# Attention values in one fp32r pass, the last branch's gates first, and wide weight splits in a hybrid encoder block

## The chip, the cores and the metric

One core of one Trainium2 chip runs the whole kernel. The metric is device microseconds of one execution, the median of several runs. Matrix products run on PE (TensorE); DVE (VectorE) and ACT (ScalarE) do the elementwise work, POOL (GpSimd) a few sums and some DMA issues, SP (SyncE) most DMA issues.

## The reference

The input is 512 tokens of width 1024 and 256 memory tokens. One layer computes

```
h = rms_norm(x);  proj = h @ w_in            # q,k,v,o,gates | na q,k,v | xa q | merge gates
y_ml = bidirectional mLSTM (4 heads of 128)
y_na = neighbourhood attention (8 heads of 64) on the 8 x 64 token grid, with a 2-D bias
y_xa = cross-attention into the memory tokens (4 heads of 128)
merged = g_ml*(y_ml @ w_br_ml) + g_na*(y_na @ w_br_na) + g_xa*(y_xa @ w_br_xa)
x = x + merged @ w_out
x = x + conv_glu_ffn(rms_norm(x))            # width 2816
return rms_norm(x)
```

All in float32. In the neighbourhood attention each token sees the 8 grid rows and a window of 16 of the 64 columns: scores, bias, softmax, and then `o = p @ v` (the "values" below).

## The kernel before

**Three passes.** A product of float32 tiles appears in the trace as two matmul records, one of fp32r tiles (a rounded format) as one. Nearly every product is made in fp32r of split operands: a number is the sum of a rounded high part and the low rest, and `mm3` (line 201) adds high by high, high by low and low by high. Activations are split by `split_act` (206: ACT copies the high part, line 208, DVE subtracts, 209).

**Weights.** All weights lie in one flat array in the order of `block_list` (53). A block is 512 KB as a rule (1024 columns on 128 partitions) and serves one projection of 24 matmuls of 512 columns (`proj`, 332). `weights(key)` (190) loads three blocks ahead on SP's queue and splits one block ahead: `emit_split` (167) makes two halves of 512 columns, each with one ACT copy (184) and one DVE subtraction (185), into four buffers of 544 columns for the high and four for the low parts.

**Order.** The kernel is written as one stream of projections; between them `step` (833) advances generators that hold the attention branches: `ml_all` (538), `xa_all` (754) and `na_all` (647), the neighbourhood attention. A compile-time scheduler orders each engine's instructions, by readiness and program order, so the engines' queues are fixed before the run. Pools are fixed too: 15 "units" of 2064 columns, 7 scratch tiles, 4 PSUM banks for projections (`mm`) and 4 for the attention (`at`).

**The branch loop (line 904).** For each of three branches, eight gate projections `("g", br, f)` (scaled by DVE at 919, tanh on ACT at 920) and four branch blocks `("br", br, fp)` of two outputs each, in the order gate, gate, branch block; gates are multiplied in at 935 and 937, summed at 938. `RATE` (31) says how many generator steps go with each: 0.85 in branch 0, 1.6 in branch 1, 0 in branch 2. `na_all` is appended when branch 1 begins; `drain` (900) runs what is left of a generator before the branch block that needs it.

**The neighbourhood attention.** Its values come out of the time-major projections at 414: in rounds c = 2 and 3 ACT copies them scaled into four scratch tiles (436), which go to a DRAM tensor `nav_d` (512 x 512) in four DMAs on POOL's queue (438). `load_vwin` (441) loads them back, once for all heads, as eight windows (4 column windows by 2 halves of the rows) of 32 partitions times 4 pieces: 32 DMAs of 64 KB on POOL's queue (448), into two units. `na_all` then has 16 tasks, one for each head and pair of column windows. Step t runs `scores` of task t (fp32r: QS and QZ by KS, 687 and 688; bias and maximum on DVE at 692; exp on ACT, 697; reciprocal; the normalising product on DVE, 699), then `values` of task t - 2, then `transposes` of task t - 1 (four float32 transposes, 705, and one copy of 128x512 out of PSUM, by ACT at 708 for even tasks and DVE at 710 for odd ones). `values` (713) makes four float32 products of 128 columns (718). After every second task `store` (720) copies the head's 64x512 result as high part (ACT, 726) and low part (DVE, 727). `prep` (654) splits q and k of two heads before every fourth task.

After the branches come the output projection (`out`), and the FFN in two halves of eleven up-blocks (`ua` with a convolution and a tanh gelu, `uu`) and eight down-blocks (`dn`).

Of the kernel before, what the change touches and what calls it, by code (L numbers as in the profile page):

```python
# [17 lines left out]
P = 128  # L18
S = 512
# [11 lines left out]
RATE = (0.85, 1.6, 0)  # L31
# [3 lines left out]
HWD = 544  # L35
# [17 lines left out]
def block_list():  # L53
# [13 lines left out]
    for br in range(3):  # L67
        for fp in range(4):
            L.append((("g", br, 2 * fp), 1024))
            L.append((("g", br, 2 * fp + 1), 1024))  # L70
            L.append((("br", br, fp), 1024))
    for f in range(8):
        L.append((("out", f), 1024))
    for hh in range(2):
# [3 lines left out]
        for f in range(8 if hh == 0 else LF):  # L78
# [3 lines left out]
            for i, n in ((0, 8), (1, 3)):  # L82
                L.append((("dn", hh, f, i), n * 128))
# [18 lines left out]
def hybrid_block(ctx, tc, xT, memT, wflat, vecs, gbias, nabias, outa, outb):  # L102
# [49 lines left out]
    def halves(i):  # L152
        n, c = BLOCKS[i][1], BCOLS[BLOCKS[i][0][0]](BLOCKS[i][0])
        k = n // c
        k0 = k if n <= HWD else (k + 1) // 2
        return c, [(0, k0)] + ([(k0, k)] if k0 < k else [])

# [9 lines left out]
    def emit_split(i):  # L167
        key, n = BLOCKS[i]
        r = raws.pop(i)
        c, hs = halves(i)  # L170
        split[i] = []
        for a, b in hs:
            m = (b - a) * c
            if key[0] == "dnl":
                h, l = lastw(4 * key[1] + a, m)
            else:
                h = wp.tile([P, HWD], F32R, tag="hi", name=nm("wh"), bufs=4)
                l = wp.tile([P, HWD], F32R, tag="lo", name=nm("wl"), bufs=4)
            for u, v in ((0, P), (P, m)) if i == 0 and a == 0 else ((0, m),):
                src = r[:, a * c + u:a * c + v]  # L180
                if i == 0 and a == u == 0:
                    V.tensor_copy(h[:, u:v], src)
                else:
                    A.activation(h[:, u:v], src, AF.Copy)  # L184
                V.tensor_tensor(l[:, u:v], src, h[:, u:v].bitcast(F32), op=ALU.subtract)  # L185
            for k in range(a, b):
                q = slice((k - a) * c, (k - a + 1) * c)
                split[i].append((h[:, q], l[:, q]))
# [223 lines left out]
    nav_d = dp.tile([S, 512], F32, name="nav_d")  # L412
    nvs = [scr() for _ in range(NT)]
    for c in range(4):
# [12 lines left out]
        for t in range(NT):  # L427
# [7 lines left out]
            else:  # L435
                A.activation(nvs[t][:, (c - 2) * 256:(c - 1) * 256], ps[:, :256], AF.Copy, scale=rc[:, t:t + 1])
    for t in range(NT):
        G.dma_start(nav_d[t * P:(t + 1) * P, :], nvs[t])
    vw = []

    def load_vwin():
        vw.extend(unit() for _ in range(2))
        nav_v = nav_d.rearrange("(a r w) f -> a r w f", a=2, r=4)
        for b in range(4):
            for hf in range(2):
                i = 2 * b + hf
                for r in range(4):
                    G.dma_start(vw[i // 4][r * 32:(r + 1) * 32, (i % 4) * 512:(i % 4 + 1) * 512],
                                nav_v[hf, r, CW[b]:CW[b] + 32, :])
    

    def vwin(b, hf, hp):
        i = 2 * b + hf
        return vw[i // 4][:, (i % 4) * 512 + hp * P:(i % 4) * 512 + (hp + 1) * P]
# [192 lines left out]
    def na_all(nq, nk, yh, yl):  # L647
# [29 lines left out]
        def scores(i, ops, bt):  # L677
# [21 lines left out]
            V.tensor_tensor(smv, smv, su.unsqueeze(2).to_broadcast([P, 2, M]), op=ALU.mult)  # L699
            return sm  # L700

        def transposes(i, sm):
# [3 lines left out]
            ptS = scr()  # L706
            if i % 2 == 0:
                A.activation(ptS, pt, AF.Copy)
            else:
                V.tensor_copy(ptS, pt)  # L710
            return ptS

        def values(i, ptS, py):

            h, bp = i // 2, i % 2
            for j in range(4):
                b, hf = 2 * bp + j // 2, j % 2
                PE.matmul(py[:, b, :], vwin(b, hf, h // 2), ptS[:, j * P:(j + 1) * P], start=hf == 0, stop=hf == 1)  # L718

# [518 lines left out]
```

## Time and profile before

| what | value |
|---|---|
| median of 3 runs | 910.26 us (910.05 to 911.16) |
| the profiled execution's own time | 909.93 us |
| its span in the trace | 908.1 us |
| PE busy | 900.4 us, 4502 matmul records |
| DVE, ACT, POOL busy | 579.5, 436.8, 107.5 us |
| DMA | 96.52 MB, 106 GB/s mean |

The 1.8 us between the execution's time and its span lie before the first and after the last instruction. A matmul's listed duration is modelled and overlaps the next one, so PE's pace is read from start to start.

### The profile page before, as it was taken

The numbers are of one execution on the slowest core, as the hardware profiler recorded it, in microseconds if no ns is written. First come the engines' busy times: TensorE is split into PE (matmuls) and PEld (weight loads), VectorE is DVE, ScalarE is ACT, GpSimd is POOL, SyncE is SP. The second block draws the span as 40 slices with busy tenths as digits, with TensorE's granted clock in tenths as the row PEclk, the third lists the DMA queues.
The fourth block names the chain that finished last, engine by engine and source line by source line (L and its number), as shares of the span: only waits on it lengthen the run. The fifth ranks groups of instructions, "written<-read, shape, count | busy, mean of one in ns | idle before, by whom it ended". The sixth has DMA issues, their size and how long they took to land.

```text
span 908.1 us, 12239 instructions
## 1 busy us (share of the span) xinstructions
PE 900.4 (99%) x4502; PEld 755.2 (83%) x4502; DVE 579.5 (64%) x1059; ACT 436.8 (48%) x884; POOL 107.5 (12%) x136
## 2 busy tenths in 40 slices
PE   9999999999999999999999999999999999999997
PEld 7899888888888888888888888888888888888887
DVE  6794656746566758885555548777733477777433
ACT  7474546755545647654334435444422244444442
POOL 4200311102040300000000221111100011111010
PEclk9999999999999999999999999999999999999999
DMA  7223543422232333232223432222233322322312
GB/s 264 96 71 119 182 119 116 156 89 82 91 119 71 114 105 127 95 117 70 93 93 117 139 116 93 93 93 92 88 96 96 116 93 93 93 93 87 119 49 93
DMA packets 33339, 96.52 MB, mean 106 GB/s; under 512 B 4344, under 2 KB 7672, under 8 KB 33280
## 3 DMA queue, kind: packets, MB, share of 16 engines
q1 hardware_dynamic: 31584, 92.32, 31.5%
q0 software_dynamic: 1408, 3.16, 1.2%
q8 instruction: 35, 0.57, 0.3%
q10 hardware_dynamic: 288, 0.27, 0.1%
q14 instruction: 24, 0.20, 0.1%
HBM read 92.57 MB, written 3.16 MB: 105 GB/s over the span
## 4 chain that ended last, share of the span: by engine, by line
PE 96%; DVE 1%; issue 1%; ACT 1%; DMA 1%; SPq 0%; POOLq 0%; POOL 0%; DVEq 0%
PE mm L202 28%; PE mm L203 28%; PE mm L204 28%; PE at L202 2%; PE at L203 2%; PE at L204 2%; PE at L580 2%; PE at L718 1%; PE at L705 1%; DMA s<-xT 1%; PE at L795 0%; PE at L688 0%; PE at L687 0%; PE at L283 0%; PE at L604 0%
## 5 line engine op out<-in xcount | busy, mean ns | idle before, releaser
L202 PE MATMUL mm<-u,wh 128*128 128x512 f32 (+1 forms) x1077 | 420.6, 391 | 0.5 <-ACT u L208 0.3
L203 PE MATMUL mm<-u,wh 128*128 128x512 f32 (+1 forms) x1077 | 417.4, 388 | 0.3 <-DVE u L209 0.3
L204 PE MATMUL mm<-u,wl 128*128 128x512 f32 (+1 forms) x1077 | 417.2, 387 | 0.0
L184 ACT ACTIVATE wh<-wr 128x512 fp32r<-128x512 f32 (+1 forms) x298 | 185.6, 624 | 285.6 <-PE mm L203 241.5
L185 DVE TENSOR_TENSOR wl<-wr,wh 128x512 fp32r<-128x512 f32 (+3 forms) x299 | 228.7, 766 | 121.4 <-ACT wh L184 114.9
L204 PEld LDWEIGHTS mm<-u,wl 128*128 128x128 f32 x1077 | 202.2, 188 | 45.2 <-DVE wl L185 0.4
L202 PEld LDWEIGHTS mm<-u,wh 128*128 128x128 f32 x1077 | 202.3, 188 | 44.2 <-ACT u L208 0.6
L203 PEld LDWEIGHTS mm<-u,wh 128*128 128x128 f32 x1077 | 202.4, 188 | 43.9 <-DVE u L209 1.3
L1111 POOL TENSOR_TENSOR s<-s,rb 128x512 f32<-128x512 f32 x22 | 29.1, 1323 | 266.4 <-DVE s L1110 258.3
L208 ACT ACTIVATE u<-s 128x512 fp32r<-128x512 f32 x34 | 21.4, 630 | 53.1 <-DVE s L1114 50.6
L964 POOL TENSOR_TENSOR acc<-acc,s 128x512 f32<-128x512 f32 x7 | 9.1, 1298 | 223.1 <-ACT s L963 223.1
L209 DVE SCALAR_TENSOR_TENSOR u<-s,u 128x512 fp32r<-128x512 f32 x34 | 23.5, 692 | 14.9 <-ACT u L208 14.6
L919 DVE TENSOR_TENSOR s<-mm,rb_x 128x512 f32<-128x512 f32 x24 | 16.6, 690 | 23.6 <-PE mm L204 23.5
L568 ACT ACTIVATE E<-R,bi 128x128 f32<-128x128 f32 x80 | 27.8, 393 | 4.2 <-POOL R L549 4.0
L369 ACT ACTIVATE s<-pad,vec 128x512 f32<-128x512 f32 x30 | 24.4, 812 | 8.3 <-DVE pad L367 8.3
L370 DVE SCALAR_TENSOR_TENSOR s<-pad,vec,s 128x512 f32<-128x512 f32 x30 | 22.5, 751 | 6.1 <-ACT s L369 6.0
L202 PE MATMUL mm<-wh,u 128*128 128x256 f32 (+1 forms) x80 | 24.5, 306 | 0.0
L203 PE MATMUL mm<-wl,u 128*128 128x256 f32 (+1 forms) x80 | 24.3, 304 | 0.0
L204 PE MATMUL mm<-wh,u 128*128 128x256 f32 (+1 forms) x80 | 24.3, 304 | 0.0
L1110 DVE SCALAR_TENSOR_TENSOR s<-s,s 128x512 f32<-128x512 f32 x22 | 15.2, 692 | 13.4 <-ACT s L1109 13.3
L371 DVE SCALAR_TENSOR_TENSOR s<-pad,vec,s 128x512 f32<-128x512 f32 x30 | 22.5, 750 | 0.7
L367 DVE TENSOR_TENSOR pad<-mm,rb 128x512 f32<-128x512 f32 x22 | 15.1, 692 | 11.6 <-PE mm L204 11.6
(261 smaller groups left out, 1003.2 us busy)
## 6 DMA issues: line engine op xcount, KB each, us to landing
wr<-wflat SPq DMA_DIRECT2D x140, 512.0 KB, 3.4
s<-xT SPq DMA_DIRECT2D x16, 256.0 KB, 4.3
nab<-nabias SPq DMA_DIRECT2D x16, 256.0 KB, 2.7
wr<-wflat SPq DMA_DIRECT2D x15, 192.0 KB, 2.4
R<-rd SPq DMA_DIRECT2D x8, 256.0 KB, 3.5
u<-nav_d POOLq DMA_DIRECT2D x32, 64.0 KB, 2.9
wr<-wflat SPq DMA_DIRECT2D x2, 544.0 KB, 3.3
s<-memT SPq DMA_DIRECT2D x4, 256.0 KB, 3.6
```

The lines of the kernel that those rows point to most:

```text
L184: A.activation(h[:, u:v], src, AF.Copy)
L185: V.tensor_tensor(l[:, u:v], src, h[:, u:v].bitcast(F32), op=ALU.subtract)
L202: PE.matmul(ps, lh, rh, start=start, stop=False)
L203: PE.matmul(ps, lh, rl, start=False, stop=False)
L204: PE.matmul(ps, ll, rh, start=False, stop=stop)
L208: A.activation(h, src, AF.Copy, scale=scale)
L209: V.scalar_tensor_tensor(l, src, scale, h.bitcast(F32), op0=ALU.mult, op1=ALU.subtract)
L369: A.activation(t1, pad[:, 0:512], AF.Identity, scale=vcol(w, i), bias=vcol(b, i))
L370: V.scalar_tensor_tensor(t1, pad[:, 1:513], vcol(w, n + i), t1, op0=ALU.mult, op1=ALU.add)
L371: V.scalar_tensor_tensor(t1, pad[:, 2:514], vcol(w, 2 * n + i), t1, op0=ALU.mult, op1=ALU.add)
L568: A.activation(E[:, i, :], src, AF.Exp, bias=bi[:, d, abs(J - s), s, h:h + 1])
L1111: G.tensor_tensor(c, c, rb2, op=ALU.mult)
```

## The change

1. **Values in one pass.** The value projections of rounds 2 and 3 are split as they leave PSUM: ACT writes the scaled high part, DVE (two instructions, one for each pair of heads) the low part, and `nav_d` becomes 512 x 1024 fp32r, laid out for each pair of heads as [high of head 0, low of head 0, low of head 1, high of head 1], 64 columns each. It goes out in eight DMAs rather than four. The transposed weights P are split too: for each of two column windows ACT copies 128x256 out of PSUM as the high part and DVE subtracts, into a tile [P high, P low] (for each of two key halves). `values` is then four fp32r matmuls of 256 columns: the 128 rows of a result are v high and v low, its columns P high and P low. `store`, now after each task, adds three of the four quadrants (one ACT copy, two DVE additions of 64x256) and splits the sum (two ACT copies and two DVE subtractions of 64x128).
2. **Values loaded by pair of heads.** `load_vwin(hp)` loads one unit for a pair of heads in 32 DMAs of 32 KB; the first pair is loaded when branch 1 begins, each next one at the step that starts the values of the pair before. 128 DMAs rather than 32.
3. **Normalisation** goes from one DVE product of 128x512 to two ACT copies of 128x256 with a scale.
4. **Last branch's gates first.** In branch 2 all eight gate projections run before the four branch blocks, into two units of their own; the rates become 0.85, 1.05 and 1.2, so that the neighbourhood attention runs through branch 1 and on through these gates.
5. **Wide splits.** `emit_split` splits a whole block with one ACT copy and one DVE subtraction, into two buffers of 1088 columns each (the first two blocks keep their pieces). The down-blocks are cut 6 + 5 rather than 8 + 3.

```diff
-RATE = (0.85, 1.6, 0)
+RATE = (0.85, 1.05, 1.2)
-HWD = 544
+KA = 6
...
+            h = wp.tile([P, BW], F32R, tag="hi", name=nm("wh"), bufs=2)
+            l = wp.tile([P, BW], F32R, tag="lo", name=nm("wl"), bufs=2)
+
+        cuts = ((0, P, n // 2, n), (0, n // 2, n))[i] if i < 2 else (0, n)
+        for u, v in zip(cuts, cuts[1:]):
+            if i == u == 0:
+                V.tensor_copy(h[:, u:v], r[:, u:v])
             else:
-                h = wp.tile([P, HWD], F32R, tag="hi", name=nm("wh"), bufs=4)
-                l = wp.tile([P, HWD], F32R, tag="lo", name=nm("wl"), bufs=4)
...
+                A.activation(h[:, u:v], r[:, u:v], AF.Copy)
+            V.tensor_tensor(l[:, u:v], r[:, u:v], h[:, u:v].bitcast(F32), op=ALU.subtract)
...
-    nav_d = dp.tile([S, 512], F32, name="nav_d")
-    nvs = [scr() for _ in range(NT)]
+    nav_d = dp.tile([S, 1024], F32R, name="nav_d")
...
+                nv = sp.tile([P, 516], F32R, tag="scr", name=nm("nv"))[:, :512]
+                nvv = nv.rearrange("p (q y d) -> p q y d", q=2, y=4)
+                pv = ps[:, :256].rearrange("p (q e d) -> p q e d", q=2, e=2)
+                A.activation(nvv[:, :, 0:4:3, :], pv, AF.Copy, scale=rc[:, t:t + 1])
+                for q in range(2):
+                    V.scalar_tensor_tensor(nvv[:, q, 1:3, :], pv[:, q], rc[:, t:t + 1], nvv[:, q, 0:4:3, :].bitcast(F32),
+                                           op0=ALU.mult, op1=ALU.subtract)
+                G.dma_start(nav_d[t * P:(t + 1) * P, (c - 2) * 512:(c - 1) * 512], nv)
...
+    def load_vwin(hp):
+        vw = unit(F32R)
...
+                    G.dma_start(vw[r * 32:(r + 1) * 32, i * 256:(i + 1) * 256],
+                                nav_v[hf, r, CW[b]:CW[b] + 32, hp * 256:(hp + 1) * 256])
...
-            V.tensor_tensor(smv, smv, su.unsqueeze(2).to_broadcast([P, 2, M]), op=ALU.mult)
+            for j in range(2):
+                A.activation(smv[:, j, :], smv[:, j, :], AF.Copy, scale=su[:, j:j + 1])
...
+            for bl in range(2):
+                w = tp.tile([P, 5, P], F32R, tag="E", name=nm("w")).rearrange("p a b -> p (a b)")
+                wv = w[:, :512].rearrange("p (k x q) -> p k x q", k=2, x=2)
+                src = pt[:, bl * 256:(bl + 1) * 256].rearrange("p (k q) -> p k q", k=2)
+                A.activation(wv[:, :, 0, :], src, AF.Copy)
+                V.tensor_tensor(wv[:, :, 1, :], src, wv[:, :, 0, :].bitcast(F32), op=ALU.subtract)
...
+            py = atps()
+            for bl in range(2):
+                for hf in range(2):
+                    c = (2 * (2 * bp + bl) + hf) * 256 + e * P
+                    PE.matmul(py[:, bl * 256:(bl + 1) * 256], vw[:, c:c + P], pp[bl][:, hf * 256:(hf + 1) * 256],
+                              start=hf == 0, stop=hf == 1)
...
+            A.activation(yv[es], pv[os, :, 0, :], AF.Copy)
+            V.tensor_tensor(yv[es], yv[es], pv[es, :, 1, :], op=ALU.add)
+            V.tensor_tensor(yv[es], yv[es], pv[es, :, 0, :], op=ALU.add)
...
+            for b in range(2):
+                A.activation(yhv[:, b], y4[:, b], AF.Copy)
+                V.tensor_tensor(ylv[:, b], y4[:, b], yhv[:, b].bitcast(F32), op=ALU.subtract)
...
+                if i % 4 == 0 and i + 4 < n:
+                    vws[i // 4 + 1] = load_vwin(i // 4 + 1)
+                store(i, values(i, pts.pop(i), vws[i // 4]))
...
+        if br == 2:
+            tgu = [unit(), unit()]
+            tgs = [gate(f, tgu[f // 4][:, f % 4 * S:(f % 4 + 1) * S]) for f in range(KT)]
         for fp in range(4):
...
+            tg = tgs[2 * fp:2 * fp + 2] if br == 2 else [gate(2 * fp + i, scr()) for i in range(2)]
             drain(tags[br])
```

110 lines of the change are left out of this document (38 added, 72 removed).

## The prediction

> **What bounds the kernel now.** I read the first page's busy times and chain first, then the stages in which the neighbourhood attention runs, then PE's own rows there.
>
> ```profile
> span 908.1 us, 12239 instructions
> PE 900.4 (99%) x4502; PEld 755.2 (83%) x4502; DVE 579.5 (64%) x1059; ACT 436.8 (48%) x884; POOL 107.5 (12%) x136
> PEclk9999999999999999999999999999999999999999
> PE 96%; DVE 1%; issue 1%; ACT 1%; DMA 1%; SPq 0%; POOLq 0%; POOL 0%; DVEq 0%
> ```
>
> PE is busy in 99% of the span at the full granted clock, and 96% of the chain that ended last is PE. A modelled busy time could hide waiting, so I check it by pace. The rows below are stages: the attention over the neighbourhood (335 to 431 us) and a stretch of the FFN (in columns: the length, then PE, PE's loads, DVE, ACT, POOL, the granted clock, DMA).
>
> ```profile
> 335.00:431.00 96.00, 95.83 (x542) 82.14 (x540) 74.29 (x189) 56.32 (x130) 0.00 (x0) 1.00 0.33 105
> 600.00:650.00 50.00, 50.00 (x218) 40.59 (x217) 38.13 (x50) 21.93 (x36) 6.24 (x5) 1.00 0.27 89
> ```
>
> In the FFN 218 matmuls of 512 columns take 50.00 us, 0.2294 us each, whatever DVE does: that is PE's own pace. PE in one step of the attention, and matmuls of 256 columns in an earlier stage:
>
> ```profile
> 353.75 0.28 PE L687 MATMUL at<-KS,QS 128*128 128x256 f32 x1
> 354.23 1.05 PE L718 MATMUL at<-s,u 128*128 128x128 f32 x8
> 355.12 0.60 PE L705 MATMUL at<-ident,s 128*128 128x128 f32 x4
> 355.47 0.48 PE L202 MATMUL mm<-u,wh 128*128 128x512 f32 x1
> 355.79 0.39 PE L203 MATMUL mm<-u,wh 128*128 128x512 f32 x1
> ```
>
> ```profile
> 84.94 0.28 PE L202 MATMUL at<-wh,u 128*128 128x256 f32 x1
> ...
> 85.76 0.28 PE L203 MATMUL at<-wl,u 128*128 128x256 f32 x1
> ```
>
> From start to start: scores 0.48 us, the eight float32 records of the values 0.89 (0.111 each), the transposes 0.35, and then the first projection matmul takes 0.32 instead of 0.23: a change from float32 back to fp32r costs 0.09. Seven fp32r matmuls of 256 columns start within 0.82 us, 0.1175 each, each with its own weight load. Of the 542 records in 335 to 431, 128 are values, 64 transposes, 64 scores, so 286 are projections: 286 x 0.2294 = 65.6, plus 16 x (0.89 + 0.35 + 0.48 + 0.09) = 29.0, makes 94.6 of 96.0 us. So even there PE waits little over 1 us. **Whatever leaves PE's queue leaves the time, and nothing else does**, as long as DVE and ACT (77% and 59% of that stage) keep up.
>
> **The change part by part.** *Values on PE.* The rows of the groups that leave or set a price:
>
> ```profile
> L718 PE MATMUL at<-s,u 128*128 128x128 f32 x128 | 17.1, 277 | 0.0
> L203 PEld LDWEIGHTS mm<-wl,u 128*128 128x128 f32 x80 | 15.1, 189 | 0.6
> L699 DVE TENSOR_TENSOR s<-s,y 128x512 f32<-128x512 f32 x16 | 11.0, 689 | 0.4
> L710 DVE COPY s<-at 128x512 f32<-128x512 f32 x8 | 5.5, 687 | 0.0
> L708 ACT ACTIVATE s<-at 128x512 f32<-128x512 f32 x8 | 4.7, 590 | 0.2
> L727 DVE TENSOR_TENSOR u<-at,u 64x512 fp32r<-64x512 f32 x8 | 5.5, 687 | 1.2 <-ACT u L726 1.1
> L726 ACT ACTIVATE u<-at 64x512 fp32r<-64x512 f32 x8 | 4.7, 584 | 0.1
> L208 ACT ACTIVATE s<-at 128x256 fp32r<-128x256 f32 x16 | 5.8, 382 | 1.5 <-DVE s L209 1.3
> L209 DVE SCALAR_TENSOR_TENSOR s<-at,s 128x256 fp32r<-128x256 f32 x16 | 6.1, 419 | 0.7 <-ACT s L208 0.2
> L436 ACT ACTIVATE s<-mm,rc_x 128x256 f32<-128x256 f32 x4 | 1.9, 465 | 0.6 <-PE mm L204 0.5
> L586 ACT ACTIVATE H<-at,y 128x128 f32<-128x128 f32 x16 | 5.7, 354 | 0.9 <-DVE y L585 0.9
> L587 DVE SCALAR_TENSOR_TENSOR H<-at,y,H 128x128 f32<-128x128 f32 x16 | 5.6, 350 | 5.0 <-ACT H L586 4.9
> L919 DVE TENSOR_TENSOR s<-mm,rb_x 128x512 f32<-128x512 f32 x24 | 16.6, 690 | 23.6 <-PE mm L204 23.5
> L920 ACT ACTIVATE s<-s,mgbh 128x512 f32<-128x512 f32 x24 | 17.4, 723 | 6.5 <-DVE s L919 6.3
> ```
>
> 128 records go: 16 x 0.89 = 14.2 us. 64 fp32r matmuls of 256 columns come: 64 x 0.1175 = 7.5 us. They stand where the old ones stood, between fp32r scores and float32 transposes, so the number of changes of format stays. **PE saves 6.7 us**, all of it on the path. Scores, transposes and projections keep their number.
>
> *DVE and ACT in the attention.* DVE loses 11.0 (normalising) + 5.5 (copy) + 5.5 (low part) = 22.0 us. It gains 32 subtractions of 128x256 at 0.419 (13.4), 32 additions of 64x256 (not shown; at most the same 0.419, 13.4) and 32 subtractions of 64x128 (at most 0.350, 11.2): 38.0, net +16.0. ACT loses 4.7 + 4.7 = 9.4. It gains 32 scaled copies at 0.465 (14.9), 32 of 128x256 at 0.382 (12.2), 16 of 64x256 at most 0.382 (6.1) and 32 of 64x128 at most 0.354 (11.3): 44.5, net +35.1.
>
> *Where that lies.* I counted the generator steps by the rates: before, the attention's 19 steps run from branch 1's first gate to the drain at branch 2's first block; after, from its second gate to the sixth gate of branch 2. The stage of 96 us held twelve weight blocks; it will hold some five gate blocks more, 5 x 24 x 0.2294 = 27.5 us, so about 96 - 6.7 + 27.5 = 117 us. DVE: 74.3 + 16.0 + 5 x (0.69 + 1.22) - 12 x 0.17 (wide splits, below) = 97.8, 84%. ACT: 56.3 + 35.1 + 5 x (0.72 + 1.05) - 12 x 0.2 = 97.9, 84%. Both under PE, but ACT rises from 59% and DVE from 77%. PE's queue is fixed at compile time, with projection matmuls between the steps; when an engine lags, PE waits at the next score, value or transpose. Now that wait is about 1 us in 96; by busier engines and a longer stage I put the new ones at **+1.0 us** (between -1.0, if the wider spacing removes them all, and +4, a quarter of a microsecond a step).
>
> *Order of branch 2.* Gates and branch blocks are the same matmuls in another order: 0 on PE. After the gates the blocks follow one another, 2.75 us for each output, with 0.69 x 3 of DVE and half a split (0.61): 2.7 us. DVE just keeps pace; the output projection needs the last low part only 21 matmuls (4.8 us) after it begins, which covers the backlog. If that cover is gone it costs one or two DVE instructions, 1.4 us.
>
> *Wide splits.* No matmul changes. One ACT copy and one DVE subtraction for a block:
>
> ```profile
> L184 ACT ACTIVATE wh<-wr 128x512 fp32r<-128x512 f32 x279 | 175.1, 629 | 262.8 <-PE mm L203 223.2 <-DMA wr<-wflat 10.2 <-issue 9.5
> L184 ACT ACTIVATE wh<-wr 128x384 fp32r<-128x384 f32 x15 | 7.8, 523 | 19.5 <-PE mm L203 16.7 <-issue 2.7
> L185 DVE TENSOR_TENSOR wl<-wr,wh 128x384 fp32r<-128x384 f32 x15 | 8.4, 558 | 15.3 <-ACT wh L184 15.2
> ```
>
> ```profile
> 558.37 0.68 DVE L185 TENSOR_TENSOR wl<-wr,wh 128x512 fp32r<-128x512 f32 x1
> ...
> 638.78 0.68 DVE L185 TENSOR_TENSOR wl<-wr,wh 128x512 fp32r<-128x512 f32 x1
> ```
>
> ```profile
> 560.74 0.39 PE L204 MATMUL mm<-u,wl 128*128 128x512 f32 x1
> ...
> 644.04 0.39 PE L204 MATMUL mm<-u,wl 128*128 128x512 f32 x1
> ```
>
> By the slopes between 384 and 512 columns, 1024 take ACT 0.63 + 4 x 0.106 = 1.05 us and DVE 0.68 + 4 x 0.13 = 1.2, saving 0.2 and 0.17 a block. A block is now ready when its whole width is, about 1.05 + 1.2 - 0.63 - 0.68 = 0.95 us after its second half was. The pairs of rows above are second halves of FFN blocks, and the matmuls that first read the same blocks: the second half ends at 559.05 and the block is used at 560.74, the tightest after the start, 1.7 us of room; the usual one ends at 639.46 and is used at 644.04, 4.6. Less 0.95 leaves 0.7 and 3.6: no wait. A down-block's first part (6 of 11 slices) may be split only when the part before it is read, five slices or 15 x 0.2294 = 3.4 us ahead of its use, and takes 0.84 + 0.95 = 1.8: 1.6 us of room. I cost wide splits at nothing, with ends of -0.5 (at the start, where ACT is full) and +2.
>
> *Values by pair of heads.* 96 more DMA issues on POOL, which has nothing else from 335 to 431 us:
>
> ```profile
> L448 POOL DMA_DIRECT2D u<-nav_d x32: 496/496/643, 254.3 to 303.3; - x32
> DMA to landing us min/median/max: 2.1/2.9/4.5
> ```
>
> A pair's 32 issues take 32 x 0.496 = 15.9 us and land 2.9 later, 18.8 us. They are issued four steps before their use: 4 / 1.05 blocks of 5.5 us and 4 x 1.4 of attention, 26.6 us. Hidden, with 8 us of room. The extra subtractions on DVE in the earlier value projections (16 of 128x128 at 0.350, 5.6 us) lie beside 22 us of matmuls there.
>
> **Sum:** 909.93 - 6.7 + 1.0 = 904.2 for an execution like the profiled one; the median of the runs shown is 0.33 higher, so 904.6.
>
> **The rivals.** *The attention starves PE (14%).* Each step now has a longer way: transposes, ACT, DVE, values, ACT, DVE twice, ACT, DVE. Against it: a whole step of projections lies between each of these, and 84% is under 100%. For it: in the chain of that stage DVE instructions stand already, the normalising product with 1.5% of the 96 us:
>
> ```profile
> by line: PE mm L204 20.1%; PE mm L203 20.0%; PE mm L202 20.0%; PE at L718 12.3%; PE at L705 6.7%; PE at L688 3.1%; PE at L687 3.0%; issue 2.1%; DVE s L699 1.5%; DVE s L937 1.4%; DVE KS L666 1.4%; DVE s L692 1.4%; DVE wl L185 1.2%; ACT s L69
> ```
>
> Each wait of W per step costs 16 W; from W = 0.42 us the 6.7 are gone, and from 0.53 the kernel is slower. With the split wholly exposed (0.382 + 2 x 0.419 = 1.2 us a step): 910.3 - 6.7 + 19.5 = 923. With W = 0.3: 908.4.
>
> *The pass is not cheaper (4%).* A weight load is listed at 0.189 us; were the 64 new matmuls paced by it, they would take 12.1 us, and the time would be 910.3 - 2.1 + 1.0 = 909.2. Against it: the rows at 84.94 start every 0.1175 us with a load each.
>
> *Weights arrive late (5%).* If the down-blocks' 1.6 us of room goes to other DVE and ACT work and 15 of them wait 0.4 us, +6: 910.6.
>
> *Value windows arrive late (3%).* From 0.74 us an issue ((26.6 - 2.9) / 32) PE waits at the first task of three pairs. At 1.0 us it would be 3 x 8.3 = 25 us: 929. Against it: the slowest issue in the trace is 0.643. The Trainium skill, page "SBUF — State Buffer", section "SBUF: two separate sides", says that DVE instructions in a two-port mode lock GpSimd out, so that it cannot write the descriptors of its DMAs. By that rule POOL's 128 issues beside a DVE at 84% would be stretched; the trace disagrees so far, since 32 issues among busy DVE work took 0.496 us in the median, and the sum goes by that row.
>
> **How the numbers follow.** Forecast 74%, rivals 14, 4, 5 and 3%. A measurement of this kernel can tell about 0.2% from no change: 908.4 to 912.1 counts as the same. Faster: the forecast and the mild end of the starving (74 + 4) = 78%. Same: 4 + 4 + 3 = 11%. Slower: 6 + 2 + 3 = 11%. The range: low end 904.6 with the waits at -1.0 instead of +1.0 and -0.5 of the splits, 902.1, rounded to 902.0; high end the forecast with +4 of waits and +2 of splits, 909.6. It leaves out the bad ends of starving and late windows and a little more.
>
> **What would show it.** Right: 64 records of 256 columns at the values' line, 0.47 us a step from start to start; PE busy lower by about 6 us, span still 99% PE; ACT and DVE at 80 to 85% from about 330 to 445 us, and PE's pace in the FFN unchanged at 0.229. Starving: gaps of PE's starts of more than 0.3 us before scores, transposes or values, and DVE or ACT in the chain. Late weights: gaps at the first matmul of a down-block. Late windows: PE waiting for a DMA at the value line. I would be wrong above all if the fixed order of the queues, and not the load, sets the waits: a 84% load doesn't show whether a copy stands behind one that waits.

## The result, and the profile after

| what | before | after |
|---|---|---|
| median, range, runs | 910.69 us (909.59 to 911.71), 22 | 911.82 us (909.89 to 913.97), 22 |
| ratio after / before | | 1.0014, 95% interval 1.0008 to 1.0021 |
| profiled execution, its span | 909.93, 908.1 us | 910.86, 909.1 us |

The kernel is 0.14% slower, some 1.3 us, which is under the 0.2% that the prediction took for no change. The forecast was 904.6 us, so the gain of nearly 6 us did not come. The first page of the profile after, the lines that answer those of before:

```profile
span 909.1 us, 12000 instructions
PE 897.0 (99%) x4438; PEld 749.7 (82%) x4438; DVE 577.1 (63%) x996; ACT 438.4 (48%) x837; POOL 162.5 (18%) x236
PEclk9999999999999999999999999999999999999999
PE 36%; DVE 1%; issue 0%; POOLq 0%; POOL 0%; DVEq 0%; ACT 0%
```

64 records have left PE and its busy time fell by 3.4 us, yet the span grew by 1.0: PE does less and waits more. The chain that ended last now covers some 38% of the span: from the end it can be followed back to 567 us, where PE waits for a weight split, and from there through DVE's queue to 563 us. The waits of PE (in each row: who waited for whom, us in total, how many times, the longest):

```profile
PE mm L194 <- DVE wl L177: 1.7, 1, 1.7
PE at L223 <- DVE warm L219: 1.2, 1, 1.2
PE mm L192 <- ACT wh L176: 1.1, 2, 0.7
PE mm L193 <- DVE u L199: 0.8, 1, 0.8
PE at L273 <- POOL acc_m L395: 0.5, 1, 0.5
PE mm L192 <- ACT u L198: 0.4, 1, 0.4
PE mm L192 <- DVE nv L431: 0.3, 1, 0.3
```

`wl` and `wh` are the wide splits, `nv` the value split in the time-major rounds, `u` the split of the activations, `acc_m` POOL's sum of the memory tokens' squares. The wait for `warm` lies at the very start and stands in every kernel here. None of these stands in the attention. Its stage, and the stretch of the FFN that the prediction used:

```profile
325.00:445.00 120.00, 119.72 (x605) 99.73 (x604) 93.92 (x245) 89.98 (x220) 31.07 (x64) 1.00 0.43 124
600.00:650.00 50.00, 50.00 (x220) 40.88 (x219) 37.15 (x41) 20.79 (x28) 6.44 (x5) 1.00 0.27 85
```

DVE is busy for 93.9 of 120 us (78%), ACT for 90.0 (75%). Two groups that the change brought (busy us and mean ns of one), and POOL's DMA issues (shortest, median and longest, ns):

```profile
L716 PE MATMUL at<-w,u 128*128 128x256 f32 x64 | 11.8, 291 | 0.2
L177 DVE TENSOR_TENSOR wl<-wr,wh 128x1024 fp32r<-128x1024 f32 x124 | 170.3, 1373 | 62.1 <-ACT wh L176 62.0
```

```profile
L443 POOL DMA_DIRECT2D u<-nav_d x128: 489/520/717, 258.5 to 394.6; - x128
```

**Where the time goes.** Every kernel here has 3241 matmul records of 512 columns, nearly all of them projections, in an order of blocks that is the same outside the branches. So the start of the n-th of them can be compared between two traces. The table shows how many us later than in the kernel before such a record starts; a row's step between two columns is what that stretch lost (+) or gained (-). The columns are times of the kernel before: 28 (first blocks), 118 (after the time-major rounds), 325 and 459 (either side of the neighbourhood attention), 522 and 586 (either side of the FFN's start), 856 (towards the end).

| kernel | 28 | 118 | 325 | 459 | 522 | 586 | 856 |
|---|---|---|---|---|---|---|---|
| after | +1.65 | +3.60 | +4.41 | -1.09 | -1.27 | +1.01 | +0.74 |
| wide_only | +1.03 | +1.71 | +2.54 | +2.80 | +2.51 | +6.33 | +4.20 |
| half_all | +0.33 | +6.56 | +6.58 | +0.46 | +0.32 | +0.16 | -0.26 |
| gates_only | +1.02 | +1.01 | +1.01 | +0.54 | +0.16 | +0.00 | -0.12 |
| values_only | +1.01 | +6.55 | +6.57 | +6.32 | +6.32 | +6.16 | +5.24 |
| half_late | +1.64 | +5.47 | +5.95 | -0.25 | -0.38 | -0.55 | -0.97 |
| half_mem2 | +1.16 | +1.16 | +1.11 | -5.11 | -5.25 | -5.43 | -5.85 |
| half_at3 | +0.98 | +0.96 | +0.98 | -5.20 | -5.34 | -5.50 | -5.91 |
| pairs_mem2 | +1.04 | +1.03 | +0.98 | +0.69 | +0.69 | +0.53 | -0.39 |
| half_mem2_dve | +0.96 | +0.94 | +0.89 | -4.83 | -4.85 | -5.00 | -5.49 |
| pieces_both | +1.65 | +6.17 | +6.98 | +1.51 | +1.33 | +1.44 | +1.17 |
| wide_mem2 | +2.34 | +3.02 | +3.86 | -1.73 | -1.91 | +0.46 | +0.18 |
| wide_mem2_pieces | +2.63 | +3.31 | +4.16 | -1.35 | -1.52 | -1.42 | -1.70 |
| pieces_all_mem2 | +2.60 | +3.28 | +4.13 | -0.68 | -0.86 | -1.27 | -1.55 |
| pieces_all_k8 | +2.45 | +3.12 | +3.98 | -0.79 | -0.97 | -1.39 | -1.66 |

Read the row of after: the attention gains 5.5 us, about the -6.7 + 1.0 of the prediction, and it is lost in other places: in the first blocks (0.9 us of it at 20 us, where wide_only loses the same; kernels with no change there stand 0.3 to 1.6 us late too, see the last section), 1.9 by the end of the time-major rounds, 0.8 at a slow pace up to 325, and 2.3 at the start of the FFN. The first theory (T1) was that the wide splits make these losses. The rivals were the order of the gates (R1), that the gain comes from the spacing and not from the fp32r pass (R2), and that only wide splits beside the new attention lose (R3).

### The profile page after: what moved, and what is told of

It reads as the page before. It is cut to its first block, busy times and chain, and to the rows that moved or that the text cites. A ratio compares the mean times of both kernels' runs of the same rounds, so it can differ in the third digit from the quotient of the medians.

```text
span 909.1 us, 12000 instructions
## 1 busy us (share of the span) xinstructions
PE 897.0 (99%) x4438; PEld 749.7 (82%) x4438; DVE 577.1 (63%) x996; ACT 438.4 (48%) x837; POOL 162.5 (18%) x236
## 3 DMA queue, kind: packets, MB, share of 16 engines
q0 software_dynamic: 7360, 6.32, 3.3%
## 5 line engine op out<-in xcount | busy, mean ns | idle before, releaser
L176 ACT ACTIVATE wh<-wr 128x1024 fp32r<-128x1024 f32 (+4 forms) x158 | 157.8, 999 | 242.4 <-PE mm L193 150.1
L177 DVE TENSOR_TENSOR wl<-wr,wh 128x1024 fp32r<-128x1024 f32 (+5 forms) x159 | 202.6, 1274 | 98.0 <-ACT wh L176 97.9
L443 POOL DMA_DIRECT2D u<-nav_d x128 | 62.6, 543 | 74.7 <-PE at L716 35.1
L975 POOL TENSOR_TENSOR acc<-acc,s 128x512 f32<-128x512 f32 x7 | 12.6, 1802 | 126.3 <-ACT s L974 126.3
L1118 ACT ACTIVATE s<-s 128x512 f32<-128x512 f32 x22 | 13.9, 632 | 41.2 <-DVE s L361 41.0
L1119 DVE SCALAR_TENSOR_TENSOR s<-s,s 128x512 f32<-128x512 f32 x22 | 15.2, 691 | 14.0 <-ACT s L1118 14.0
L1121 DVE SCALAR_TENSOR_TENSOR s<-s,s 128x512 f32<-128x512 f32 x22 | 15.2, 691 | 13.3 <-ACT s L1120 13.3
L361 DVE SCALAR_TENSOR_TENSOR s<-pad,vec,s 128x512 f32<-128x512 f32 x30 | 22.5, 750 | 0.8
```

The lines of the kernel that those rows point to most:

```text
L176: A.activation(h[:, u:v], r[:, u:v], AF.Copy)
L177: V.tensor_tensor(l[:, u:v], r[:, u:v], h[:, u:v].bitcast(F32), op=ALU.subtract)
L361: V.scalar_tensor_tensor(t1, pad[:, 2:514], vcol(w, 2 * n + i), t1, op0=ALU.mult, op1=ALU.add)
L443: G.dma_start(vw[r * 32:(r + 1) * 32, i * 256:(i + 1) * 256], nav_v[hf, r, CW[b]:CW[b] + 32, hp * 256:(hp + 1) * 256])
```

## Experiments

Every time below is the median of a kernel's runs, and each ratio is to the kernel before in the same set of runs.

### One part at a time

**wide_only**: the kernel before with part 5 (the core of its edit).

```diff
-                h = wp.tile([P, HWD], F32R, tag="hi", name=nm("wh"), bufs=4)
+            h = wp.tile([P, BW], F32R, tag="hi", name=nm("wh"), bufs=2)
```

> The kernel before with part 5 alone (wide splits, two buffers of 1088 columns, down-blocks cut 6 + 5); values, gates and rates as before. Theory T1 (the whole-block splits cost the time that the values pass gains: about 1.6 us in the first blocks, 2.7 us at the start of the FFN): slower than before by 3 to 5 us, about 914.5 us, with PE waiting for the high and low weight parts (lines of the wide split) at the first blocks and at the first up-blocks. Rival R1 (the order of the gates or the new POOL DMAs make the losses, the width is innocent): within 1 us of before, 910 to 911.5. Rival R3 (only the pairing of wide splits with the new attention work loses): within 1 us of before too, and the FFN start without a wait.

Measured: 914.99 us (914.12 to 915.92), ratio 1.0045 (1.0032 to 1.0057). T1 held; R1 and R3 fell, since there are no new gates or values here. Part 5 costs 4 us by itself.

**half_all**: the kernel after without part 5.

```diff
-            h = wp.tile([P, BW], F32R, tag="hi", name=nm("wh"), bufs=2)
+                h = wp.tile([P, HWD], F32R, tag="hi", name=nm("wh"), bufs=4)
```

> The kernel after with part 5 undone (half-width splits in four buffers of 544 columns, down-blocks cut 8 + 3); the values pass, loading by pair, normalisation on ACT and gates first stay. T1: faster than after by 3.5 to 5 us, about 907.5 us; the waits at the first blocks and at the start of the FFN are gone, the 1.3 us at 100 us (PE waits behind POOL's sums and DVE's value split) stays. R1: within 1 us of after, 911 to 912.

Measured: 909.62 us (908.50 to 911.19), ratio 0.9986 (0.9977 to 0.9995). Faster than after by 2.5 us by the ratios, not by 4: the FFN's loss is gone (its row: 0.32 to 0.16), but 6.2 us are now lost before 118. What was 1.9 us in after is worse without the wide splits, so a second cause stands there.

**gates_only**: the kernel before with part 4, the order of blocks and the rates.

```diff
-RATE = (0.85, 1.6, 0)
+RATE = (0.85, 1.05, 1.2)
```

> The kernel before with part 4 alone (last branch's gates first, the rates 0.85, 1.05 and 1.2). T1: nothing, 910 to 911.5 us, since the matmuls are the same and only their order differs. Rival R1 (the new order delays what stands at the FFN's start): slower by 2 us or more, 913. Rival R2 (the 5.6 us that the branches gained come from the wider spacing of the attention, not from the fp32r pass): faster by 3 us or more, 907 or less.

Measured: 909.40 us (908.63 to 910.58), ratio 0.9985 (0.9977 to 0.9994). A gain of 1.4 us where I expected none, by the table half a microsecond of it in the attention and as much after it. R1 fell, and the spacing alone is not worth the 5.6 us of R2.

**values_only**: the kernel before with parts 1 to 3, half widths, the old gates and rates.

```diff
-RATE = (0.85, 1.05, 1.2)
+RATE = (0.85, 1.6, 0)
```

> The kernel before with parts 1, 2 and 3 (values in one fp32r pass, loads by pair of heads, normalisation on ACT); half-width splits, gates in pairs and the rates of before. The attention then runs inside branch 1 at 1.6 steps a projection. T1: faster than before by 3 to 6 us, 905 to 907.5 us; the closer spacing may cost up to 2 us of waits in the attention. Rival R2 (the gain needs the spacing, because ACT and DVE are full at the old rate): 909 or more, with PE waiting for DVE or ACT at the values and transposes.

Measured: 915.23 us (914.41 to 916.93), ratio 1.0052 (1.0039 to 1.0065). T1 missed by 9 us. Two things went wrong: 5.5 us lost before 118, as in half_all, and only 0.25 us gained in the attention. R2 has a point; pairs_mem2, below, takes it up without the first loss.

### The stall at 100 us

In half_all PE stands still as the time-major rounds end. Its two longest waits, and two stages (in each row: from and to, length, PE, PE's loads, DVE, ACT, POOL, granted clock, DMA):

```profile
PE at L284 <- POOL acc_m L406: 2.4, 1, 2.4
PE mm L203 <- DVE nv L442: 1.3, 1, 1.3
```

```profile
98.70:103.60 4.90, 1.25 (x7) 0.95 (x5) 2.41 (x8) 3.55 (x10) 2.64 (x3) 0.72 0.01 2
103.60:107.20 3.60, 3.59 (x9) 2.83 (x10) 3.59 (x9) 0.17 (x1) 2.71 (x5) 0.50 0.66 189
```

PE works 1.25 of 4.9 us, and then for 3.6 us at half the clock: nine matmuls, 0.427 us apart instead of 0.23. Its instructions in time (start, duration, engine and line; in brackets the idle time ahead and who ended it):

```profile
99.47 1.82 POOL L406 TENSOR_TENSOR acc_m<-acc_m,s 128x256 f32<-128x256 f32 x2 [0.87 <-ACT u L209]
99.69 1.54 ACT L440 ACTIVATE nv<-mm,rc_x 128x256 fp32r<-128x256 f32 x4
...
101.34 1.01 PE L284 MATMUL at<-ones,acc_m 128*128 128x1 f32 x4 [2.41 <-POOL acc_m L406]
...
102.39 0.16 DVE L286 TENSOR_SCALAR y<-at 128x2 f32<-128x2 f32 x1 [2.49 <-PE at L284]
102.47 0.47 DVE L210 SCALAR_TENSOR_TENSOR u<-s,vec,u 128x256 fp32r<-128x256 f32 x1
...
102.86 1.38 DVE L442 SCALAR_TENSOR_TENSOR nv<-mm,rc_x,nv 128x128 fp32r<-128x128 f32 x5
...
103.61 0.77 PE L203 MATMUL mm<-u,wh 128*128 128x512 f32 x1 [1.26 <-DVE nv L442]
```

This is a ring of fixed queues. PE's next instruction is the product of `acc_m`, which POOL has not summed. DVE's next one needs that product, and behind it on DVE stands the value split `nv`. The split reads the projection banks (`mm`), and PE's next projection needs one of those. In the kernel before the copy on ACT freed the banks, the projections went on, and the `acc_m` product came amid them:

```profile
109.10 0.60 PE L492 MATMUL at<-ident,lfc 128*100 128x128 f32 x4
...
115.09 0.50 PE L283 MATMUL at<-ones,acc_m 128*128 128x1 f32 x4
```

Because the banks come free later, the scheduler has put `lfc` and `acc_m` ahead of the projections, at a time when `acc_m` is not ready. Theory T2: this order makes the loss. The rival R4: DVE and ACT simply have too much to do there.

**half_late**: half_all, the product of `acc_m` asked for four projections later.

```diff
-        if f == 2:
-            mrc = rstd_cols(macc, M, "m")
-        if f == 3:
-            mrb = rstd_row(mrc, M, "m")
         step(RB)
     for f in range(4):
         ps = proj(("o", f), XH, XL)
...
+        if f == 1:
+            mrc = rstd_cols(macc, M, "m")
+        if f == 2:
+            mrb = rstd_row(mrc, M, "m")
         step(RB)
```

> The kernel half_all with one thing moved: the sum over the memory's squares (the product of ones by acc_m, and the row made of it) is asked for four projections later, in the loop of the o projections. In half_all PE stands from 98.66 to 103.61 us: 2.4 us for POOL's acc_m, 1.3 for DVE's value split, whose place on DVE is behind the scaling that needs the acc_m product; then nine matmuls start every 0.427 us at a granted clock of 0.50. Theory T2 (a queue order: PE, DVE and POOL hold one another up through the early acc_m product; the value split alone would free the bank at about 100.8 us): faster than half_all by 3 to 5 us, 905 to 907 us, about 2 us of wait for the value split left, and no slow matmuls. Rival R4 (the value split itself is too much work for DVE and ACT there, the acc_m product is innocent): within 1 us of half_all, 909 to 910.

Measured: 908.90 us (906.16 to 909.34), ratio 0.9981 (0.9972 to 0.9990). Little: 0.5 us below half_all by the ratios, and their intervals overlap. The wait for `acc_m` is gone, but PE now waits 2.5 us for the split at one time, and the half clock follows again:

```profile
PE mm L203 <- DVE nv L442: 2.5, 1, 2.5
```

```profile
99.60:102.70 3.10, 0.65 (x6) 0.40 (x5) 2.98 (x7) 3.10 (x9) 1.92 (x3) 1.00 0.01 3
102.70:106.30 3.60, 3.56 (x9) 2.82 (x10) 3.59 (x9) 0.83 (x2) 2.67 (x5) 0.53 0.66 193
```

DVE and ACT are full in that gap (2.98 and 3.10 of 3.10 us): the memory tokens' splits stand ahead of `nv`. So the `acc_m` product alone was not it: T2's size was wrong by some 3 us, and R4 is right that the work there is dense.

**half_mem2**: half_all, the memory tokens' part one round earlier.

```diff
-        if c == 3:
+        if c == 2:
             mem_part()
```

> The kernel half_all with the splitting and squaring of the memory tokens (16 ACT copies and 16 DVE subtractions of 128x256, four squares, POOL's sums) one time-major round earlier, ahead of round 2 and not of round 3; nothing else is changed. T2: ACT and DVE reach the value split of round 3 in time, the compile-time order leaves the transposes of lfc and the acc_m product amid the xaq projections as in the kernel before, no wait at 100 us: faster than half_all by 5.5 to 6.5 us, about 903.6 us, that is 7 us below before. R4: the wait stays, or comes in round 2: 908 or more. Rival R5 (the attention's 6 us were paid by the stall, as a rested clock, and go with it): 909.

Measured: 904.14 us (903.02 to 904.69), ratio 0.9934 (0.9922 to 0.9947). **half_at3**: half_all, the last round in the attention's banks.

```diff
-        pss = [(mmps if c % 2 else atps)() for _ in range(NT)]
+        pss = [(mmps if c == 1 else atps)() for _ in range(NT)]
```

> The kernel half_all with one thing changed: round 3 of the time-major projections accumulates in the four attention banks (at), as rounds 0 and 2 do, so that the xaq projections find the projection banks (mm) free and don't wait for DVE's value split. T2 in its form that the bank held by the value split starts it all: the wait at 100 us is gone, 904 us, as far below half_all as the kernel with the earlier memory splits; the at banks may now wait for round 2's split, up to 2 us. If the load on DVE and ACT is the cause (R4): 908 or more.

Measured: 904.14 us (903.54 to 904.44), ratio 0.9937 (0.9924 to 0.9949). Either edit removes the whole stall: to do the same work earlier, or to leave it where it is and take away the bank that couples it to PE. The second decides between T2 and R4: in half_at3 DVE and ACT have as much to do as in half_all, and it costs nothing.

```profile
98.00:103.00 5.00, 5.00 (x28) 4.23 (x28) 4.94 (x12) 4.48 (x10) 3.39 (x5) 1.00 0.08 29
```

DVE is busy for 4.94 of these 5 us and ACT for 4.48, and PE works through all of them; `lfc` and the `acc_m` product come later, at 110 and 116 us, amid the projections as in the kernel before. It is the bank, held behind a queue, that makes the load count; R5 fell too. These two, with half_mem2_dve below, are the fastest kernels of the case. All the waits of PE that the view lists for half_mem2:

```profile
PE at L234 <- DVE warm L230: 1.2, 1, 1.2
PE mm L203 <- ACT u L209: 0.4, 1, 0.4
PE at L727 <- DVE w L716: 0.2, 1, 0.2
```

### The attention's spacing

**pairs_mem2**: half_mem2 without part 4.

```diff
-RATE = (0.85, 1.05, 1.2)
+RATE = (0.85, 1.6, 0)
```

> The kernel half_mem2 with part 4 undone: gates in pairs in the last branch, the rates 0.85, 1.6 and 0, so that the attention runs inside branch 1. If the fp32r pass needs the wider spacing (ACT and DVE full at 1.6 steps a projection, as the profile of values_only has it, which gained only 0.25 us in the attention): 909.5 to 910.5 us, about the kernel before, and the 6 us of half_mem2 come from parts 1 and 4 together. If values_only lost them only through the clock or order that its stall at 100 us left behind: 904 to 905 us.

Measured: 909.30 us (908.24 to 910.21), ratio 0.9984 (0.9974 to 0.9993): 4.6 us slower than half_mem2 by the ratios. In the table the attention gains 0.3 us, not 6.2. So R2 is half right: the gain is the fp32r pass's, but only at the wider spacing. With the attention in branch 1 alone the waits eat it, mostly at the values (L727) and transposes (L708):

```profile
PE at L727 <- DVE w L716: 1.2, 4, 0.4
PE at L708 <- ACT s L702: 1.1, 3, 0.5
PE at L727 <- issue: 0.5, 1, 0.5
```

These sum to 2.8 of the 5.9 us. The remainder lies in waits too short for this view: adding up, record by record, by how much PE's starts between the columns 325 and 459 come later than the usual spacing of such a pair of records gives some 9 to 10 us in pairs_mem2 and 3 to 4 in half_mem2, about 6 more; some 3.5 of these stand before values and 2.1 before transposes. **half_mem2_dve**: half_mem2 without part 3.

```diff
-            for j in range(2):
-                A.activation(smv[:, j, :], smv[:, j, :], AF.Copy, scale=su[:, j:j + 1])
+            V.tensor_tensor(smv, smv, su.unsqueeze(2).to_broadcast([P, 2, M]), op=ALU.mult)
```

> The kernel half_mem2 with part 3 undone: the normalisation as one DVE product of 128x512 instead of two ACT copies of 128x256. If the load decides, DVE goes from about 84% to over 90% in the attention and PE waits some 1 to 3 us more: 905 to 907 us. If the spacing leaves room on both engines: the same, 903.6 to 904.6 us.

Measured: 904.61 us (903.84 to 905.31), ratio 0.9932 (0.9919 to 0.9944). Where the normalisation runs makes no difference at this spacing.

### What it is in the wide splits that costs time

**pieces_both**: the kernel after, the first eight blocks and the FFN's first six in two instructions each, into the wide buffers.

```diff
+        if i >= 2 and (key[0] in ("mlq", "mlk") or key[0] in ("ua", "uu") and key[1] < 3):
+            cuts = (0, (n // c + 1) // 2 * c, n)
```

> The kernel after (wide splits, two wide buffers) with the first eight blocks (mlq, mlk) and the first six blocks of the FFN (ua and uu of 0 to 2) split in two instructions for each engine, each half as wide, into the same wide buffers; all else wide. T1 in its form that the width of the instruction is what is late (a block ready only as a whole, a long instruction in the fixed order): faster than after by 2.5 to 4 us, 908 to 909.3, the waits at 8, 20, 542 and 565 us gone. Rival R6 (the two whole buffers are what is late, since a half can't be refilled before the whole block is read; the instructions' width is innocent): within 0.7 us of after, 911 to 912.5.

Measured: 911.20 us (909.23 to 912.44), ratio 1.0011 (1.0002 to 1.0020), as R6 had it; but the table shows that the sum hides two things. The FFN's start lost 0.1 us and not 2.3, as T1 had it; and this profiled execution lost 4.5 between 28 and 118, with eight slow matmuls behind the stall, where that of after lost 1.9 and had none. A stall that sometimes brings the half clock blurs the comparison, so the next kernels have it removed.

**wide_mem2**: the kernel after, `mem_part()` at `c == 2`, and nothing else.

> The kernel after with one thing changed: the memory tokens are squared and split one time-major round earlier, as in the kernel half_mem2; the wide splits stay. T2: the stall at 100 us goes (1.8 us in the profiled execution of after, up to 4.5 where the clock falls behind it as in other kernels), so faster than after by 2 to 4.5 us, 907.5 to 910 us; the 2.3 us at the start of the FFN stay, with a gap of about 2.1 us on PE there. Beside half_mem2 (904.1) it shows what the wide splits cost in all: 3.5 to 6 us. If the wide splits cost nothing but through the stall: 904 to 905.

Measured: 910.26 us (908.72 to 910.62), ratio 0.9993 (0.9984 to 1.0001). Two results. The stall costs the kernel after 1.9 us (1.0014 less 0.9993). And beside half_mem2 (0.9934) **the wide splits cost 5.4 us by the ratios**, 6.0 in the table: 1.2 at the start, 1.6 up to 325, 0.6 in the attention, 2.5 at the FFN's start, 0.1 after it. The three longest waits at projections are all for wide splits or for work that stands behind them:

```profile
PE mm L194 <- DVE wl L177: 1.8, 1, 1.8
...
PE mm L193 <- DVE u L199: 0.8, 1, 0.8
PE mm L192 <- ACT wh L176: 0.4, 1, 0.4
```

The longest one, seen in the kernel after (DVE's order ahead of the late low part):

```profile
559.65 1.05 ACT L176 ACTIVATE wh<-wr 128x1024 fp32r<-128x1024 f32 x1
560.27 0.69 DVE L1125 TENSOR_TENSOR s<-mm,s 128x512 f32<-128x512 f32 x1 [1.19 <-POOL s L1122]
...
562.96 0.69 DVE L1125 TENSOR_TENSOR s<-mm,s 128x512 f32<-128x512 f32 x1 [0.80 <-POOL s L1122]
...
565.44 0.74 DVE L361 SCALAR_TENSOR_TENSOR s<-pad,vec,s 128x512 f32<-128x512 f32 x1
566.10 1.22 DVE L177 TENSOR_TENSOR wl<-wr,wh 128x1024 fp32r<-128x1024 f32 x1
...
567.37 0.50 PE L194 MATMUL mm<-u,wl 128*128 128x512 f32 x1 [1.73 <-DVE wl L177]
```

The high part is done at 560.70. The low part starts 5.4 us later, behind eight other instructions in DVE's order, two of which wait for POOL. One long instruction has one place in the order. In half_mem2 the same block is split by two short ones at two places, among the same instructions, and PE first reads its low part at 560.91:

```profile
554.81 0.69 DVE L186 TENSOR_TENSOR wl<-wr,wh 128x512 fp32r<-128x512 f32 x1
...
558.16 0.68 DVE L186 TENSOR_TENSOR wl<-wr,wh 128x512 fp32r<-128x512 f32 x1
```

**wide_mem2_pieces**: wide_mem2 with the pieces of pieces_both.

> The kernel wide_mem2 with the first eight blocks and the first six blocks of the FFN split in two instructions for each engine, into the same wide buffers. T1 in its form that the long instruction is late at the FFN's start: faster than wide_mem2 by 2 to 4 us, 905 to 906.5 us, no gap on PE between 540 and 590 us; what is left above half_mem2 (904.1), about 1 us, is the slower pace between 140 and 325 us. R6 (the two whole buffers are late, the instructions are innocent): within 0.7 us of wide_mem2.

Measured: 908.47 us (906.99 to 909.71), ratio 0.9974 (0.9965 to 0.9983). T1 for the FFN's start: its loss goes from 2.4 to 0.1 us. But 3.6 us above half_mem2 remain by the ratios. **pieces_all_mem2**: the same pieces in every block but the last spare ones; against half_mem2 only the two wide buffers, the down-blocks' cut and those spare blocks differ.

> The kernel wide_mem2 with every block (but the last three projections' spare blocks) split in two instructions for each engine, each as wide as in the kernel before, into the two wide buffers. Against half_mem2 (904.1 us) only the buffers differ (two of 1088 columns, not four of 544, so that no half is free before the whole block is read) and the down-blocks' cut (6 + 5). If the instructions' width makes the 6 us of the wide splits: 904 to 905. If the two whole buffers make what the pieces at the start and in the first FFN blocks did not remove (wide_mem2_pieces, 908.5): 907.5 to 909. In between, it divides the two.

Measured: 908.58 us (907.08 to 909.20), ratio 0.9975 (0.9966 to 0.9983). The short instructions gain nothing more: **the two whole buffers cost the other 3.7 us** (0.9975 less 0.9934), with the cut 6 + 5. At the first blocks it can be seen how. ACT splits the next block in half_mem2 at 15.45 us, as soon as one half buffer has been read. In pieces_all_mem2 it starts at 18.16, when PE is through the whole block, although its instructions are as short:

```profile
15.45 0.63 ACT L185 ACTIVATE wh<-wr 128x512 fp32r<-128x512 f32 x1 [1.01 <-PE mm L204]
```

```profile
18.16 0.64 ACT L178 ACTIVATE wh<-wr 128x512 fp32r<-128x512 f32 x1 [3.61 <-PE mm L195]
...
23.04 0.50 PE L195 MATMUL mm<-u,wh 128*128 128x512 f32 x1 [1.43 <-DVE u L201]
```

Behind the late split on ACT and DVE stand the splits of x (200, 201), for which PE waits 1.43 us. **pieces_all_k8**: the same with the old cut of the down-blocks.

```diff
-KA = 6
+KA = 8
```

> The kernel pieces_all_mem2 with the down-blocks cut 8 + 3 as in the kernel before: against half_mem2 only the buffers differ. If the cut 6 + 5 costs or gains anything it shows here: I expect the same as pieces_all_mem2 within 0.7 us, since no gap stands on PE at the down-blocks in wide_mem2.

Measured: 910.58 us (909.23 to 912.85), ratio 1.0000 (0.9991 to 1.0009), 2.3 us slower than pieces_all_mem2 and not the same. Against half_mem2 only the buffers and the spare blocks of the last three projections differ here, and it stands 6.0 us above it. With two whole buffers a first part of eight slices leaves three slices of time for the next split. That alone is not enough: the table shows no loss up to 856, though all earlier down-blocks are cut in the same way. PE waits at the last ones, where the whole split of a spare block, which has waited 3.8 us for its DMA, stands ahead on ACT:

```profile
858.11 1.06 ACT L178 ACTIVATE u<-wr 128x1024 fp32r<-128x1024 f32 x1 [3.80 <-DMA wr<-wflat]
...
859.73 0.50 PE L194 MATMUL mm<-u,wh 128*128 128x512 f32 x1 [0.42 <-ACT wh L178]
...
861.08 0.50 PE L196 MATMUL mm<-u,wl 128*128 128x512 f32 x1 [0.60 <-DVE wl L179]
```

So the cut 6 + 5 is a part of the change that works, and with half buffers the cut 8 + 3 does as well.

## Why the prediction was wrong

**Values on PE: right.** 64 records instead of 128, at 0.118 us from start to start (the median); in half_mem2 the attention gains 6.2 us of the forecast 6.7, and 5.5 in after. Counted at the usual spacing of its records, without waits, that stretch has shrunk by 6.6 us. **Waits in the attention: right in size** (0.5 of the 1.0 in half_mem2). DVE and ACT came out at 78 and 75%, below the 84% of the working. **POOL's 96 more DMA issues: right**, 0.520 us each in the median against 0.496, and no wait of PE for a window is listed in after. The rule of the Trainium skill that the prediction named (page "SBUF — State Buffer", section "SBUF: two separate sides": DVE instructions in a two-port mode lock GpSimd out of writing descriptors) is not seen in them, beside a DVE that is busy for 78% of that stage. The prediction took such rows for evidence against the rule. They don't test it, since no run here shows which of DVE's instructions, if any, are in such a mode.

**Order of branch 2: 0 on PE was too low** by 1.4 us (gates_only), and the step missed its true worth: without it the attention gains 0.3 us from the fp32r pass and not 6.2 (pairs_mem2). That a busier, closer spacing starves PE was the prediction's first rival; the wider spacing is what kept it away.

**Wide splits: the step that failed.** "I cost wide splits at nothing", the prediction says, with +2 us as the bad end. They cost 5.4 us by the ratios and 6.0 in the table (wide_mem2 beside half_mem2): 1.6 by the single long instructions and 3.7 by the whole buffers. The working took the end of a half's split in the trace of before, added 0.95 us for the width, and compared it with the first use: 0.7 us of room at the tightest block. That takes for granted that the split keeps its place in the queues. It does not: at the start of the FFN the whole low part begins 5.4 us after its high part is done, behind eight others. The late block is not even the one picked as the tightest but the next one, whose second half ended in the kernel before at 564.21 us and which was first read at 566.34, 2.1 us of room. And it counted only how long the instructions take, not what two whole buffers do: a half buffer came free at half a block, a whole one at its end. The rival "weights arrive late" had the size (+6), by luck, since it had the wrong place: the down-blocks, the only place where the change had taken care of it.

**The value projections: costed at nothing, 1.9 us.** The extra subtractions "lie beside 22 us of matmuls there" is true of their load, and half_at3 shows that the load was no matter. What it missed is that these instructions hold the banks which the next projections need. The prediction closed on this very possibility, that the fixed order and not the load sets the waits, and gave it no price.

With these two losses away, as in half_mem2, 904.14 us stand beside the forecast 904.6. That they lie so close is luck in part, since the order of branch 2 brought 1.4 us that the sum had at 0. Put together, half_mem2's gain of 6.0 us by the ratio, the 5.4 of the wide splits and the 1.9 of the stall make the 1.3 us by which the kernel after is slower.

**Open.** In the traces (pieces_all_mem2 beside half_mem2) the whole buffers cost 1.4 us in the first blocks, 1.6 between 28 and 325 us and 1.4 in the attention, more than half of the last in short waits before values. The 1.6 come with no gap on PE: between 140 and 320 us the matmuls of 512 columns start 235.1 to 235.4 ns apart in the mean in kernels with wide buffers, and 233.9 to 234.2 in those with halves. Where the tiles lie in memory may do it; that wasn't tried. Loading by pair of heads (part 2) has no run of its own.

## What to carry to other kernels

Where PE is the bound and the queues are fixed at compile time, price an edit on another engine not by its busy time but by what it holds while it waits its turn: a PSUM bank, or a weight buffer of which half could have come free. Merging two instructions into one saves 0.2 us of engine time and takes away a place in the order, and whole buffers come free later than half ones; compare the order of the queues at the tightest block before calling it free. And try the parts alone: this change held a part worth 6.2 us in the attention, one that made it possible, one that made no difference, and one that took nearly all of it back.

## What was not expected of the hardware

A short gap on PE can cost more than itself. Behind one, seven to nine matmuls of 512 columns started 0.427 us apart at a granted clock of about 0.5, which makes 8 x 0.2 = 1.6 us more than their pace of 0.23. From the traces: wide_only and after have nearly the same gap at the same place of the FFN. In wide_only two matmuls start 2.19 us apart and the half clock follows, in after 2.13 and it does not. The rows of wide_only first, then of after, ending in the granted clock, DMA share and GB/s:

```profile
568.90:571.40 2.50, 0.70 (x3) 0.28 (x2) 2.50 (x4) 1.43 (x2) 0.00 (x0) 1.00 0.00 0
571.40:575.40 4.00, 4.00 (x12) 3.12 (x12) 2.55 (x4) 0.78 (x2) 1.28 (x1) 0.57 0.72 229
```

```profile
565.20:567.40 2.20, 0.47 (x3) 0.04 (x2) 2.20 (x4) 1.19 (x2) 0.00 (x0) 1.00 0.00 0
567.40:571.40 4.00, 4.00 (x18) 3.29 (x19) 2.45 (x4) 1.02 (x2) 1.29 (x1) 1.00 0.62 200
```

Twelve matmuls in 4 us against eighteen. In wide_mem2 the gap of 2.17 us cost no clock, in half_late 2.76 did. In pieces_both one of 1.85 us did, with only four matmuls of one column right behind it: from 104.30 us on eight started 0.427 us apart. The Trainium skill, page "TensorE: Matmul & The Clock Gate", section "HAM oscillation — how this bites in real kernels", gives as its rule that PE should have no idle gaps over about 3.4 us. The traces agree on the half rate and the length of the slow stretch, some 3.4 to 3.6 us, and not on the bound: 2.19 us of gap were enough, where 2.13 and 2.17 were not. The same page of the Trainium skill, section "What's actually happening", says that the window is free-running, which would fit a matter of chance; what decides wasn't tried. It may be why the 22 runs of after spread over 4.1 us, and the 22 of before, with no such gap, over 2.1.

The start of the kernel has such a stretch too. Between about 6 and 9 us six to ten matmuls start 0.427 us apart in gates_only, values_only, half_mem2 and most others, with the granted clock listed as 1.00 all the same; in before, after, wide_only, half_all and pieces_both they don't. It makes most of the 1 us in column 28 of the kernels whose first blocks are unchanged.
